# Dividing an attention's rows by their softmax sums behind the value products

## The chip, the core and the metric

The kernel runs on one core of a Trainium2 chip. The core has a matrix engine (TensorE, PE in the profile, with PEld for its weight loads), a vector engine (DVE), an activation engine (ACT), GpSimd (POOL) and a queue that issues most of the DMAs (SP); ACT and POOL issue some too. Sixteen DMA engines move the data. The metric is the device time of one execution in microseconds (us); the kernel before takes 2106.4 us, the median of 3 runs (2104.5 to 2107.51).

## The reference

One encoder layer in float32 is applied to two sequences, a prompt of 1024 tokens and a sample of 512 tokens, with a model width of 1024:

```python
z  = rmsnorm(x) @ w_in          # q_A k_A v_A | q_B k_B v_B | gate_A gate_B
mix = (sigmoid(gate_A) * (o_A @ w_proj_a) + sigmoid(gate_B) * (o_B @ w_proj_b)) @ w_out
h  = x + mix
h  = h + relu(rmsnorm(h) @ w_up)**2 @ w_down
y  = rmsnorm(h)
```

Branch A, which is what changes, is grouped-query attention over all tokens: 8 query heads of 64 columns share 2 key/value heads.

```python
s = einsum('bqkgd,bskd->bkgqs', q, k) * 64**-0.5
p = softmax(s, axis=-1)
o_A = einsum('bkgqs,bskd->bqkgd', p, v)
```

Branch B is attention in a 2-D neighbourhood with a learned bias, and is not touched.

## The kernel before

The two sequences are run one after the other by `run`, first the sample (`NB` = 1 block of 512 queries, tiles named with s0 in the program), then the prompt (`NB` = 2). The multilayer perceptron follows for both together. Matrix products are made in a three-pass form: each operand is split into a high part, rounded to the fast float32 format of TensorE, and a low rest.

For each of the two key/value heads `g`, a stage `phR` makes queries, keys and values, and a stage `phA` makes the attention of the four query heads of that group. Its unit of work is `u = (h, qb)`, a head and a block of 512 queries; there are 8 units in the sample and 16 in the prompt, 24 in all. A unit goes through these steps:

- `s_tile(u, j)`, four times for 128 queries each: two (sample) or four (prompt) matmuls into a score tile in PSUM (lines 801 and 802; there are two such tiles, pool `pbig`), the negated row maximum on DVE (L804), the exponential on ACT with the row sum as a second result (L811), the reciprocal of the sum on DVE (L813), and the division of the whole tile by its sum on POOL (L814). The tile `p` is 128 queries by T keys.
- The tiles are turned, so that keys lie on partitions. In the sample and in the prompt's first query block `t_chunk` does it with four TensorE transposes per 128 keys into a PSUM tile (L838), from which ACT copies the high part (L841) and DVE subtracts it to get the low part (L842). In the prompt's second query block `turn_a` transposes 32 x 32 blocks on DVE (L856) and writes the tile to DRAM (L857, SP), `fetch_a` fetches it turned (L882, SP), and `cut_a` splits it on ACT (L887) and POOL (L889, two halves).
- `pv(u, kc, hi, lo)` multiplies the values with a chunk of 128 keys (lines 825 and 826). The value operand `vhl` holds high and low parts side by side, so its result `o` has 128 rows: 64 of the high part and 64 of the low part, by 512 queries.
- `finish_o`, after the last chunk: ACT copies the lower 64 rows (L484), DVE adds the upper 64 (L494), and `put` stores the sum to the DRAM tensor `oad` by a DMA issued from ACT's queue (L439).

The output of `finish_o` has queries along its 512 columns, while the sums have queries on partitions. `oad` is read again much later, in the projection of branch A (`load_o`, L969).

Work of other kinds is drawn in between by a generator `fill`: `fill.pull(1)` takes one step of the gate products (L214, `gpss`), whose weights are loaded on SP (L247) into three buffers of `rawp` and split on ACT and DVE (L201, L208). The loops of the stage write the order of these calls out by hand; the planner of the tile framework then fixes the order of instructions on each engine from that order, from the dependences, and from costs that it assumes. Once built, every engine's queue is in order: an instruction, or the issue of a DMA, that waits holds all that stands behind it on the same engine.

Of the kernel before, what the change touches and what calls it, by code (L numbers as in the profile page):

```python
# [11 lines left out]
F32 = mybir.dt.float32  # L12
# [3 lines left out]
ALU = mybir.AluOpType  # L16
AX = mybir.AxisListType

P = 128
D = 1024  # L20
NC8 = D // P
HD = 64
# [39 lines left out]
def encoder(ctx: ExitStack, tc: tile.TileContext, xs, outs, w):  # L62
    nc = tc.nc
    dram = ctx.enter_context(tc.tile_pool(name="dram", bufs=1, space=bass.MemoryType.DRAM))
    cst = ctx.enter_context(tc.tile_pool(name="cst", bufs=1))
    sml = ctx.enter_context(tc.tile_pool(name="sml", bufs=8))
# [26 lines left out]
    def mm(name):  # L93
        return pmm.tile([P, 512], F32, tag="mm", name=name)

    def big(name):
        return pbig.tile([P, 1024], F32, tag="big", name=name)
# [325 lines left out]
    def run(tr, nxt, first):  # L423
        N, x, T, NT, NB = tr.N, tr.x, tr.T, tr.NT, tr.NB
        xh, xl = tr.xh, tr.xl
        rows = T // GRID_W
# [4 lines left out]
        oad = dram.tile([4 * P, T], F32, name=f"oad{N}")  # L431
# [5 lines left out]
        def put(dst, src):  # L437
            if slot_no[0] is None:
                nc.scalar.dma_start(dst, src)  # L439
            else:  # L440
                later_put.append((slot_no[0], dst, src))
# [27 lines left out]
                    put(dst[c * P : (c + 1) * P, tb * 512 : tb * 512 + 512], sg)  # L469
                    yield  # L470

        def finish_o(o, n, dst, pool, nm, parts=None):

            both = len(o.shape) == 3
            cols = 2 * n if both else n
            t = pool.tile([P, cols], F32, tag="ot", name=f"ot_{nm}", bufs=2 if cols == 512 and both else 3)
            c, b = t[0:HD, 0:n], t[0:HD, cols - n : cols]
            if both:
                tv = t[0:HD].rearrange("p (i q) -> p i q", i=2)
                nc.scalar.activation(tv, o[HD:P], AF.Copy)  # L480
                nc.vector.tensor_tensor(tv, o[0:HD], tv, op=ALU.add)
                o = b
            else:
                nc.scalar.activation(c, o[HD:P, :n], AF.Copy)  # L484
                o = o[0:HD, :n]
            if parts is not None:
                hi, lo, ps = parts
                b = t[ps, cols - n : cols]
                nc.vector.tensor_tensor(b, o, c, op=ALU.add)
                nc.scalar.activation(hi, b, AF.Copy)  # L490
                op = nc.vector.tensor_tensor(lo, b, hi.bitcast(F32), op=ALU.subtract)
                last_sum[:] = [op.ins]
                return
            nc.vector.tensor_tensor(b, o, c, op=ALU.add)  # L494
            put(dst, b)


# [41 lines left out]
        for g in range(2):  # L539
            with phase(f"phR{N}_{g}") as ph:  # L540
# [175 lines left out]
                for tt in range(NT):  # L716
                    tb, j = divmod(tt, 4)
                    nm = f"{N}_{g}_{tt}"
# [17 lines left out]
                    op = nc.sync.dma_start(rt, w["rope"][tt * P : (tt + 1) * P])  # L736
# [51 lines left out]
                setup_bias()  # L788
            with phase(f"phA{N}_{g}") as ph:
                units = [(h, qb) for h in range(4) for qb in range(NB)]  # L790
                PP = {}

                def s_tile(u, j):
                    h, qb = u
                    nm = f"{N}_{g}_{h}_{qb}_{j}"
                    q0 = (qb * 4 + j) * P
                    lhs = qT[h % 2][:, h // 2, q0 : q0 + P]
                    s = big(f"s{nm}")[:, :T]
                    for kb in range(NB):
                        ks = slice(kb * 512, kb * 512 + 512)  # L800
                        nc.tensor.matmul(s[:, ks], lhs, kT[:, 0, ks], start=True, stop=False)
                        nc.tensor.matmul(s[:, ks], lhs, kT[:, 1, ks], start=False, stop=True)  # L802
                    nm_ = sml.tile([P, 1], F32, tag="nm", name=f"nm{nm}")
                    nc.vector.tensor_reduce(nm_, s, axis=AX.X, op=ALU.max, negate=True)  # L804
                    p = ph.tile([P, T], F32, tag="P", name=f"p{nm}", bufs=8)
                    l = sml.tile([P, 1], F32, tag="l", name=f"l{nm}")
                    to, of = p, s
                    if NB == 2 and qb == 1:
                        to = p.rearrange("p (b k i) -> p k b i", b=4, i=32)
                        of = s.rearrange("p (k i b) -> p k b i", b=4, i=32)  # L810
                    op = nc.scalar.activation(to, of, AF.Exp, bias=nm_, accum_out=l)  # L811
                    rl = sml.tile([P, 1], F32, tag="rl", name=f"rl{nm}")
                    nc.vector.reciprocal(rl, l)  # L813
                    nc.gpsimd.tensor_scalar(p, p, rl, 1.0, op0=ALU.mult, op1=ALU.mult)  # L814
                    PP[u, j] = p
                    return op.ins

                o_of = {}

                def pv(u, kc, hi, lo):  # L820
                    h, qb = u
                    if kc == 0:
                        o_of[u] = mm(f"o{N}_{g}_{h}_{qb}")
                    o = o_of[u]
                    nc.tensor.matmul(o, vhl[:, kc, :], hi, start=(kc == 0), stop=False)
                    nc.tensor.matmul(o, vhl[:, kc, :], lo, start=False, stop=(kc == NT - 1))
                    if kc == NT - 1:
                        r0 = (g * 4 + h) * HD
                        finish_o(o, 512, oad[r0 : r0 + HD, qb * 512 : qb * 512 + 512], ph, f"A{N}_{g}_{h}_{qb}")

                queue = []
                LAG = 2
# [1 line left out]
                def t_chunk(u, kc):  # L834
                    h, qb = u
                    pt = mm(f"pT{N}_{g}_{h}_{qb}_{kc}")
                    for j in range(4):
                        nc.tensor.transpose(pt[:, j * P : (j + 1) * P], PP[u, j][:, kc * P : (kc + 1) * P], ident)  # L838
                    hi = ph.tile([P, 512], F32R, tag="pth", name=f"pth{N}_{g}_{h}_{qb}_{kc}", bufs=3)
# [5 lines left out]
                def next_pv():  # L845
                    if len(queue) > LAG:
                        pv(*queue.pop(0))
# [3 lines left out]
                def turn_a(u, j):  # L851
                    h, qb = u
                    if u not in PD:
                        PD[u] = dram.tile([4, P, T], F32, name=f"ta{N}_{g}_{h}")
                    p = PP.pop((u, j))
                    nc.vector.transpose(p, p)  # L856
                    nc.sync.dma_start(PD[u][j], p)  # L857

                def step_s(u, j):
                    end = s_tile(u, j)  # L860
                    while due:
                        turn_a(*due.pop(0))
                    if u[1]:
                        due.append((u, j))
                    return end
# [25 lines left out]
                if NB == 2:  # L891
# [6 lines left out]
                    for h in range(4):  # L898
                        u, nn, nd = (h, 1), (h + 1, 0), (h + 1, 1)
# [27 lines left out]
                else:  # L927
                    for j in range(4):
                        ends = s_tile(units[0], j)
                        last_exp[:] = [ends]  # L930
                        fill.pull(2)
                    for ui, u in enumerate(units):
                        h, qb = u
# [18 lines left out]
                for item in queue:  # L952
                    pv(*item)
# [85 lines left out]
        with phase(f"phB{N}") as ph:  # L1039
# [4 lines left out]
            n = len(units)  # L1044
# [211 lines left out]
            def v_unit(u):  # L1256
# [27 lines left out]
                if h < 6:  # L1284
                    finish_o(o, nq, obd[h * HD : h * HD + HD, j * nq : (j + 1) * nq], ph, f"B{nm}")
                else:
                    if not oX3:
                        oX3.append(slot([P, 2, T], F32R, f"oX{N}_1_3"))
                    ps = slice(64 * (h % 2), 64 * (h % 2) + 64)
                    hi, lo = (oX3[0][ps, i, j * nq : (j + 1) * nq] for i in range(2))  # L1290
                    finish_o(o, nq, None, ph, f"B{nm}", (hi, lo, ps))
# [18 lines left out]
            for i in range(n + 4 - NB):  # L1310
                if moved:
                    slot_no[0] = i
                if i < n - 8:
                    f = (5 if i < 2 else 2 + i % 2) if NB == 1 else 5 - (i % 6 == 5)
                else:
                    f = 3 if NB == 1 else 8
# [4 lines left out]
                if i < n:  # L1321
# [4 lines left out]
                    h, j = units[i]  # L1326
# [57 lines left out]
        with phase(f"phG{N}") as ph:  # L1384
            oX = load_o(1) + oX3
            wos = [None, None]
            parts = []
# [22 lines left out]
            for c in range(NC8):  # L1410
# [3 lines left out]
                for tb in range(NB):  # L1414
# [4 lines left out]
                    nm = f"{N}_{c}_{tb}"  # L1419
# [30 lines left out]
            for half in range(2):  # L1450
                wo = wos[half]
                hc = slice(half * 512, half * 512 + 512)
                for tt in range(NT):
                    tb, j = divmod(tt, 4)
                    nm = f"{N}_{half}_{tt}"
                    r0 = tr.t0 + tt * P
# [16 lines left out]
                    if half == 0 and NB == 1:  # L1473
# [4 lines left out]
                        o = o4[tt]  # L1478
                    else:
                        o = mm(f"op{nm}")  # L1480
# [27 lines left out]
                    if half == 1:  # L1508
# [12 lines left out]
                        else:  # L1521
# [10 lines left out]
                            if 3 <= tt <= 5:  # L1532
                                j = tt - 3
# [495 lines left out]
    for i, tr in enumerate(trunks):  # L2029
        run(tr, trunks[i + 1] if i + 1 < len(trunks) else None, i == 0)  # L2030
# [66 lines left out]
```

## Time and profile before

| | |
|---|---|
| median of 3 runs | 2106.4 us (2104.5 to 2107.51) |
| profiled execution | 2105.4 us |
| its span in the profile | 2103.6 us |
| POOL busy over the span | 445.6 us (21%) |
| attention of branch A, sample | within 50 to 155 us of the span |
| attention of branch A, prompt | within 440 to 600 and 640 to 765 us |

A row of the profile's groups names the line of the kernel, the engine, the operation, what it writes and reads (`out<-in`), the shapes, the count, the busy time in us and the mean of one in ns; behind that stands how long the engine was idle just before it and what ended that time. In a list of waits each row names who waited for whom, with the total in us, how often, and the longest. In a timeline each row begins with the start and the length in us. Trailing letters of a name stand for numbers left out: `ps` is any probability tile, `pTs` its transpose in PSUM, `os` the product with the values, `hqs` a quarter of a fetched tile, `ptls` and `pths` the low and high parts.

### The profile page before, as it was taken

What the parts mean: (1) busy time and instruction counts of PE and PEld (TensorE: products, weight loads), DVE (VectorE), ACT (ScalarE), POOL (GpSimd) and SP (SyncE); (2) the same over time, 40 slices, a digit from 0 to 9 for tenths busy, and PEclk for the clock granted to TensorE, in tenths of its full rate; (3) what the DMA queues carried; (4) which work ended last, traced back from release to release, by engine and by line L of the source; (5) the groups of instructions that cost most, each with busy time, mean ns of one, the idle gap of its engine ahead of it and who ended that gap; (6) DMA issues with size and microseconds to landing.
All of it is one profiled execution on the core that took longest, in us unless ns stands there. A gap on an engine that the chain in (4) does not pass through costs nothing. (4 is left out here: it accounts for less than half of the span.)

```text
span 2103.6 us, 31314 instructions
## 1 busy us (share of the span) xinstructions
PE 2072.8 (99%) x10615; PEld 1809.0 (86%) x10615; DVE 1477.5 (70%) x2761; ACT 1142.2 (54%) x2455; POOL 445.6 (21%) x510
## 2 busy tenths in 40 slices
PE   9999999999999999999999999999999999999998
PEld 8887878987797778888888999999999988888886
DVE  6665786778648747778854877787777777669563
ACT  6664753667566745566423556565556634334442
POOL 2232310338435823543102100011000000000000
PEclk9999999999999999999999999999999999999999
DMA  6437557557626866877553666478445899788561
GB/s 193 136 101 209 158 165 253 182 135 191 171 65 182 208 170 198 235 225 219 181 182 131 196 195 206 153 240 223 145 155 161 283 342 348 214 273 277 159 209 61
DMA packets 406758, 406.45 MB, mean 193 GB/s; under 512 B 97599, under 2 KB 333767, under 8 KB 406599
## 3 DMA queue, kind: packets, MB, share of 16 engines
q1 hardware_dynamic: 368119, 339.16, 52.8%
q10 hardware_dynamic: 31328, 45.11, 6.4%
q0 software_dynamic: 7152, 20.19, 3.5%
q8 instruction: 84, 1.38, 0.3%
q14 instruction: 75, 0.61, 0.1%
HBM read 291.06 MB, written 114.10 MB: 193 GB/s over the span
## 5 line engine op out<-in xcount | busy, mean ns | idle before, releaser
L214 PE MATMUL dn<-wd,ah 128*128 128x512 f32 x1248 | 384.4, 389 | 0.0
L214 PEld LDWEIGHTS dn<-wd,ah 128*128 128x128 f32 x1248 | 234.2, 188 | 48.7
L214 PE MATMUL dn<-wd,al 128*128 128x512 f32 x624 | 242.8, 389 | 0.0
L1571 ACT ACTIVATE ah<-ar 128x512 fp32r<-128x512 f32 x168 | 104.1, 627 | 203.3 <-PE dn L214 184.3
L214 PE MATMUL gpss<-xs_0h,w_gs 128*128 128x512 f32 x512 | 186.1, 400 | 0.3 <-DVE w_gs L208 0.2
L1572 DVE TENSOR_TENSOR al<-ar,ah 128x512 fp32r<-128x512 f32 x168 | 113.9, 686 | 71.6 <-ACT ah L1571 64.7
L214 PE MATMUL ud<-B,A 128*128 128x384 f32 x768 | 143.6, 334 | 0.7 <-DVE c L1689 0.7
L214 PE MATMUL uc<-B,A 128*128 128x384 f32 x768 | 143.7, 334 | 0.0
L214 PE MATMUL ua<-B,A 128*128 128x384 f32 x768 | 138.8, 334 | 0.0
L214 PEld LDWEIGHTS dn<-wd,al 128*128 128x128 f32 x624 | 117.1, 188 | 24.2
L214 PEld LDWEIGHTS ud<-B,A 128*128 128x128 f32 x768 | 134.0, 188 | 1.1 <-DVE c L1689 1.1
L214 PEld LDWEIGHTS uc<-B,A 128*128 128x128 f32 x768 | 134.1, 188 | 0.2 <-ACT A L1571 0.2
L214 PEld LDWEIGHTS ua<-B,A 128*128 128x128 f32 x768 | 133.7, 188 | 0.2
L180 POOL TENSOR_TENSOR rs_f<-ms_f,mhalf 128x1 f32<-128x1 f32 x6 | 4.0, 667 | 590.7 <-DVE ms_f L176 590.7
L811 ACT ACTIVATE ps<-ss,nms 128x1024 f32<-128x1024 f32 (+1 forms) x96 | 93.4, 973 | 56.4 <-DVE nms L804 46.1
L814 POOL TENSOR_SCALAR ps<-ps,rls 128x1024 f32<-128x1024 f32 (+1 forms) x96 | 97.8, 1019 | 123.6 <-DVE rls L813 105.8
L214 PE MATMUL ops<-wh_os,mgs 128*128 128x512 f32 x384 | 119.5, 391 | 0.0
L804 DVE TENSOR_REDUCE nms<-ss 128x1 f32<-128x1024 f32 (+1 forms) x96 | 99.4, 1038 | 21.7 <-PE ss L802 20.6
L214 PEld LDWEIGHTS gpss<-xs_0h,w_gs 128*128 128x128 f32 x512 | 96.2, 189 | 18.7 <-DVE w_gs L208 0.7
L214 PE MATMUL gpss<-xs_0l,w_gs 128*128 128x512 f32 x256 | 101.2, 395 | 0.0
L1571 ACT ACTIVATE A<-S 128x512 fp32r<-128x512 f32 x128 | 75.9, 624 | 31.7 <-DVE S L1634 22.9
L214 PE MATMUL gpss<-xs_1h,w_gs 128*128 128x512 f32 x256 | 90.8, 393 | 0.0
(299 smaller groups left out, 5160.9 us busy)
## 6 DMA issues: line engine op xcount, KB each, us to landing
ar<-ud SPq DMA_DIRECT2D x120, 512.0 KB, 5.3
br<-in_w_mlp_down_dram SPq DMA_DIRECT2D x72, 512.0 KB, 5.3
rawu<-in_w_mlp_up_dram SPq DMA_DIRECT2D x64, 512.0 KB, 4.1
ud<-c ACTq DMA_DIRECT2D x128, 192.0 KB, 2.6
raw_gs<-in_w_in_dram SPq DMA_DIRECT2D x32, 512.0 KB, 3.9
tas<-ps SPq DMA_DIRECT2D x32, 512.0 KB, 3.1
hqs<-tas SPq DMA_DIRECT2D x32, 512.0 KB, 6.1
ud<-cs SPq DMA_DIRECT2D x64, 192.0 KB
```

The costliest lines, as they stand in the source:

```text
L180: op = nc.gpsimd.tensor_tensor(r[:, :n], m[:, :n], mhalf[:, :n], op=ALU.pow)
L214: op = nc.tensor.matmul(out, a, b, **kw)
L804: nc.vector.tensor_reduce(nm_, s, axis=AX.X, op=ALU.max, negate=True)
L811: op = nc.scalar.activation(to, of, AF.Exp, bias=nm_, accum_out=l)
L814: nc.gpsimd.tensor_scalar(p, p, rl, 1.0, op0=ALU.mult, op1=ALU.mult)
L1571: nc.scalar.activation(hi, src, AF.Copy)
L1572: nc.vector.tensor_tensor(lo, src, hi.bitcast(F32), op=ALU.subtract)
```

## The change

The tiles are no longer divided. The four row sums of a unit go into one tile of four columns, one reciprocal is made of it, and it is written to a DRAM tensor of 4 x 128 values on SP. When the unit's value products begin, the 512 reciprocals are fetched to each of 64 partitions, also on SP, into a tile with two buffers in the sample and one in the prompt. `finish_o` multiplies the sum by that tile on POOL before the store. Branch B calls `finish_o` without it.

```diff
-        def finish_o(o, n, dst, pool, nm, parts=None):
+        def finish_o(o, n, dst, pool, nm, parts=None, scale=None):
...
             nc.vector.tensor_tensor(b, o, c, op=ALU.add)
+            if scale is not None:
+                nc.gpsimd.tensor_tensor(b, b, scale, op=ALU.mult)
             put(dst, b)
...
-                PP = {}
+                PP, L4, rd = {}, {}, {}
...
                     p = ph.tile([P, T], F32, tag="P", name=f"p{nm}", bufs=8)
-                    l = sml.tile([P, 1], F32, tag="l", name=f"l{nm}")
+                    if j == 0:
+                        L4[u] = ph.tile([P, 4], F32, tag="l4", name=f"l{nm}", bufs=4)
+                    l = L4[u][:, j : j + 1]
...
                     op = nc.scalar.activation(to, of, AF.Exp, bias=nm_, accum_out=l)
-                    rl = sml.tile([P, 1], F32, tag="rl", name=f"rl{nm}")
-                    nc.vector.reciprocal(rl, l)
-                    nc.gpsimd.tensor_scalar(p, p, rl, 1.0, op0=ALU.mult, op1=ALU.mult)
                     PP[u, j] = p
+                    if j == 3:
+                        rl = ph.tile([P, 4], F32, tag="r4", name=f"rl{nm}", bufs=3)
+                        nc.vector.reciprocal(rl, L4.pop(u))
+                        rd[u] = dram.tile([4, P], F32, name=f"rd{nm}")
+                        nc.sync.dma_start(rd[u].rearrange("j p -> p j"), rl)
                     return op.ins
...
-                o_of = {}
+                o_of, rb_of = {}, {}
...
                     if kc == 0:
                         o_of[u] = mm(f"o{N}_{g}_{h}_{qb}")
+                        rows = ph.tile([P, 512], F32, tag="rb", name=f"rb{N}_{g}_{h}_{qb}", bufs=3 - NB)
+                        nc.sync.dma_start(rows[0:HD], rd.pop(u).rearrange("j p -> (j p)").partition_broadcast(HD))
+                        rb_of[u] = rows[0:HD]
...
                     if kc == NT - 1:
                         r0 = (g * 4 + h) * HD
-                        finish_o(o, 512, oad[r0 : r0 + HD, qb * 512 : qb * 512 + 512], ph, f"A{N}_{g}_{h}_{qb}")
+                        finish_o(o, 512, oad[r0 : r0 + HD, qb * 512 : qb * 512 + 512], ph, f"A{N}_{g}_{h}_{qb}", None, rb_of.pop(u))
```

## The prediction

> **What bounds the kernel now.** I read the page's head first, then busy time by stage, then the waits of the weight loads, then single stretches of the timeline.
>
> ```profile
> span 2103.6 us, 31314 instructions
> PE 2072.8 (99%) x10615; PEld 1809.0 (86%) x10615; DVE 1477.5 (70%) x2761; ACT 1142.2 (54%) x2455; POOL 445.6 (21%) x510
> ...
> 50.00:155.00 105.00, 103.45 (x572) 87.82 (x571) 70.92 (x155) 68.78 (x194) 30.93 (x42) 1.00 0.39 120
> 440.00:600.00 160.00, 154.07 (x789) 126.14 (x789) 112.40 (x178) 104.48 (x233) 88.59 (x79) 1.00 0.63 162
> 640.00:765.00 125.00, 120.62 (x571) 93.19 (x570) 88.24 (x132) 81.17 (x128) 76.75 (x64) 1.00 0.76 199
> ```
>
> TensorE (PE) is busy nearly everywhere, at full granted clock (1.00, the column ahead of the DMA share). So nothing that another engine saves is worth anything unless it ends a wait of PE. The change lies in branch A's attention, which falls in the three stretches shown (columns: length, then PE, PEld, DVE, ACT, POOL): 50 to 155 us is the sample, the other two are the prompt's two key groups. The rest is not touched. What matters is what PE waits for there:
>
> ```profile
> PE pTs L838 <- POOL ps L814: 2.3, 7, 0.4
> ...
> PEld pTs L838 <- DVE ptls L842: 8.5, 10, 1.8
> PEld ss L801 <- ACT ps L811: 8.1, 20, 1.3
> PEld pTs L838 <- POOL ps L814: 7.8, 16, 0.8
> ...
> PEld os L826 <- DVE ptls L842: 3.8, 7, 0.8
> PEld pTs L838 <- DVE ot_As L494: 2.6, 8, 0.8
> ```
>
> The columns are total us, times, longest. The change takes away what stands in the third PEld row: transposes of the probabilities wait for POOL's division (L814). The matmul row above it gives the same wait 2.3 us, the weight loads give it 7.8. Two stretches show how much time is lost:
>
> ```profile
> 505.70 0.48 PE L825 MATMUL os<-pths,vhls 128*128 128x512 f32 x1
> 506.34 0.19 PEld L826 LDWEIGHTS os<-ptls,vhls 128*128 128x128 f32 x1 [0.48 <-DVE ptls L842]
> 506.34 0.50 PE L826 MATMUL os<-ptls,vhls 128*128 128x512 f32 x1 [0.16 <-DVE ptls L842]
> 506.68 0.40 PE L214 MATMUL gpss<-xs_0h,w_gs 128*128 128x512 f32 x1
> 506.91 0.40 PE L214 MATMUL gpss<-xs_0l,w_gs 128*128 128x512 f32 x1
> ...
> 59.18 0.40 PE L214 MATMUL gpss<-xs_0h,w_gs 128*128 128x512 f32 x1
> 59.70 0.14 PEld L838 LDWEIGHTS pTs<-ident,ps 128*128 128x128 f32 x1 [0.57 <-POOL ps L814]
> 59.71 0.33 PE L838 MATMUL pTs<-ident,ps 128*128 128x128 f32 x1
> ```
>
> Undisturbed, the next matmul starts 0.23 us later (506.68 to 506.91). In the first stall 0.64 passed (505.70 to 506.34): 0.41 lost, where the weight load shows a wait of 0.48 and the matmul 0.16. In the second 0.53 passed: 0.30 lost, of 0.57 shown by the load and nothing by the matmul. Together 0.71 of 1.05, so I count a weight-load wait at 0.68 of its length. The Trainium skill (Perfetto Trace Analysis, Identifying the Most-Contended Engine) says that matmul busy time misleads, because matmuls are pipelined, and that the busy share of the weight loads is to be used; these two stalls agree that the matmul row shows too little, but the load row shows too much. By the matmul row the first term below would be 2.3 us, by the load row 7.8.
>
> **The change, part by part.** Times are set against the profiled execution: 2105.4 us with a span of 2103.6. The median of the runs is 2106.4, so 1.0 is added at the end.
>
> *POOL's division goes out.* These are the steps behind it:
>
> ```profile
> L814 POOL TENSOR_SCALAR ps<-ps,rls 128x1024 f32<-128x1024 f32 (+1 forms) x96 | 97.8, 1019 | 123.6 <-DVE rls L813 105.8
> ...
> L814 POOL TENSOR_SCALAR ps<-ps,rls x96: 691/1119/2002, 53.1 to 731.8; 128x1024 f32<-128x1024 f32 x64, 128x512 f32<-128x512 f32 x32
> ...
> L813 DVE RECIPROCAL rls<-ls x96: 120/152/166, 52.8 to 730.9; 128x1 f32<-128x1 f32 x96
> ...
> DVE rls L813 <- ACT ps L811: 14.7, 16, 1.4
> DVE ps L856 <- POOL ps L814: 10.5, 14, 1.4
> ```
>
> POOL loses 97.8 us, which is worth nothing by itself. Each tile becomes ready for its transposes one reciprocal (0.152) and one pass (1.019 on average, 0.69 in the sample) earlier. The longest stall on it is 0.8, so with the order of PE as it is, every one of these 16 stalls ends: 7.8 x 0.68 = 5.3 us. What is late next is the exponential itself (L811), which comes no earlier. Bounds: 0, if PE's order is planned anew and the transposes are put forward by as much as the chain is shorter, and 5.3. I take 5.3.
>
> *96 reciprocals become 24* of four columns. DVE loses 72 x 0.152 = 10.9 us of work, three quarters of the 14.7 us in which it stood before a reciprocal until the exponential's sum was there (11.0), and most of the 10.5 us in which its block transposes (L856, the prompt's second query block) waited for POOL. That is up to 32.4 us for the engine on which PE waits most in these stages: 8.5 + 3.8 + 2.6 = 14.9 us of load waits, 10.1 after the factor. Per unit (a head and 512 queries, 24 in all) DVE gains 1.35 and PE loses 0.42 to it. Bounds: 0 (the freed time lies behind the stalls) to 10.1. I take half, 5.1, as only relief in front of a stall helps. The 8.1 us for score tiles held by an exponential (5.5 after the factor) I leave at 0, since ACT's own work stays; 5.5 is the bound.
>
> *A product on POOL behind the sum* (24 times, 64 x 512, two inputs). The nearest row is POOL's other two-input pass, the hi/lo cut of the prompt:
>
> ```profile
> L889 POOL TENSOR_TENSOR hqs<-hqs x48: 1271/1292/1737, 470.8 to 739.6; 128x512 fp32r<-128x512 f32 x48
> ...
> L439 ACTq DMA_DIRECT2D oads<-ot_As x24: 452/453/503, 75.1 to 756.8; - x24
> ...
> L484 ACT ACTIVATE ot_As<-os x8: 593/594/596, 670.0 to 755.5; 64x512 f32<-64x512 f32 x8
> ```
>
> It is as long in the free dimension, so 1.29 us each, 31 us in all on an engine that has just lost 98. No matmul reads the product: it goes to DRAM and is read again by the projection much later. But the store sits in ACT's queue (L439), and now waits for POOL instead of DVE; behind it on ACT are exponentials and the hi copies, for which PE waits. The 1.29 itself is a known step that the plan can put other ACT work in front of. What it may miss is that POOL is in a pair of cuts. In the last stretch the cuts are 32 x 1.292 = 41 of 125 us, a third of the time; a third of 16 prompt units with half of a pair (1.3) left is 6.9 us of ACT held. ACT is busy 81.17 of 125 (0.65), so that share is pushed on, and 0.68 of it counts: 3.0 us. In the sample POOL has nothing else and I take 0. Bounds: 0, and a whole pair each time (below, second rival).
>
> *Two DMAs per unit on SP*: 512 single values of 4 bytes out to DRAM, then 2 KB to each of 64 partitions.
>
> ```profile
> vss<-vds SPq DMA_DIRECT2D x128, 32.0 KB, 2.0
> ...
> hqs<-tas SPq DMA_DIRECT2D x32, 512.0 KB, 6.1
> ...
> oads<-ot_As ACTq DMA_DIRECT2D x24, 128.0 KB, 4.2
> ...
> 57.48 0.69 ACT L811 ACTIVATE ps<-ss,nms 128x512 f32<-128x512 f32 x1
> ...
> 72.95 0.59 ACT L484 ACTIVATE ot_As<-os 64x512 f32<-64x512 f32 x1
> ...
> SPq L1073 <- DMA zgs<-sgs: 20.3, 8, 8.6
> ...
> PEld gpss L214 <- DVE w_gs L208: 0.7, 1, 0.7
> ```
>
> The smallest transfers land in 2.0 us. The fetch of 512 KB in runs of 256 bytes is 2048 packets, 128 for each of 16 engines, in 6.1, so a small packet is about (6.1 - 2.0) / 128 = 0.032 us, an estimate. 512 values are 32 per engine, 1.0 us: the row lands after 3.0, the 128 KB to 64 partitions after 4.2 more, 7.2 in all. The first unit's last exponential ends at 58.2 and its sum begins at 73.0, so 14.8 us stand ready. In the prompt, where there is one buffer for the row, the next fetch waits for the product of the unit before; sums come (755.5 - 670.0) / 7 = 12.2 us apart, and product, store slot and fetch are about 6. On the 16 DMA engines 8 units in the last stretch add 8 us to 95 of 125, and the rows a little more: 0.76 becomes about 0.85. The SP queue is in order: a write waits for the reciprocal, a fetch for the write's landing, and behind them stand gate weights, the prompt's block transfers and fetches. Waits of SP for a landing were 2.5 us on average (20.3 / 8). PE waited for gate weights 0.7 us in all, and the three raw buffers ahead of them are the cover; without it 24 holds of 2.5 would be 60 us on SP. I take 0 and let the range carry the rest. The tiles at a stage's end come free some 2 us later, before work that PE does not wait for now: 0.
>
> *Sum*: 2105.4 - 5.3 - 5.1 + 3.0 = 2098.0, and with 1.0 for the median **2099.0 us**.
>
> **The rivals.**
>
> *No change.* The order of PE is planned anew; transposes move forward until they wait for the exponential as they waited for POOL, and DVE's freed time lies behind its stalls. For it: PE already stops 20 times for the exponential in the rows above. Against it: the stalls on POOL are short (0.49 on average) beside what is saved (0.8 to 1.2). The terms vanish and the hold stays: 2106.4 + 3.0 = 2109.4, at best 2102.
>
> *Slower: ACT held at the store.* In each of the 16 prompt units the product comes behind a full pair of cuts, 2 x 1.29 = 2.58 us: 41.3 us of ACT held, x 0.65 x 0.68 = 18.3 instead of 3.0, so 2099.0 + 15.3 = 2114.3. It cancels the gain of 10.4 from 1.5 us of mean hold per prompt unit (10.4 / (16 x 0.65 x 0.68)), and makes the kernel measurably slower from 2.1. For it: POOL is in order and the cuts come in pairs. Against it: POOL loses nearly half of its work in this stage (32 passes of 1.12 out of 76.75), and the store at present is issued with no wait of its own.
>
> *Larger gain.* DVE's relief ends all its stalls: 2106.4 - 5.3 - 10.1 + 3.0 = 2094.0, and if scores stop waiting too and nothing is held, 2106.4 - 20.9 = 2085.5.
>
> *The row comes late.* This needs a packet of 4 bytes to take (14.8 - 2.0 - 4.2) / 32 = 0.27 us, eight times the estimate. At 0.4 it is late by 4.2 us; in the eight sample units alone, x 0.66 x 0.68, that is 15 us, so about 2114. The Trainium skill (DMA: Bandwidth & Descriptors, Rules for kernel authors) speaks against this write: a strided last dimension becomes one descriptor per element, and its Specifications add that transfers under 512 bytes are done by read-modify-write. No run here shows such a write yet.
>
> That the change doesn't do what it says can be excluded: the 96 passes leave the program.
>
> **How the numbers follow.** About 0.2% (4.2 us) is what a measurement of this kernel can tell from no change. Forecast (2094 to 2102) 0.42; larger gain 0.16; no change (2102 to 2110.6) 0.23; held store 0.16; late row 0.03. So faster 0.58, same 0.23, slower 0.19. The range 2086 to 2112 leaves out the last of the larger gain (0.04) and most of the two slower cases (0.14). The forecast's own range is 2094 to 2102.
>
> **What would show it.** Right: no wait of the transposes on POOL, weight-load waits on DVE in the three stretches down by about half, POOL's time down by some 65 us, PE's order in the stretches much the same. Wrong: the wait of transposes on the exponential grown by what the other lost; ACT's next instruction behind an L439 store late with POOL in its cuts; the 64-partition row landing after the sum; gate matmuls waiting for their weights.

## The result, and the profile after

The changed kernel takes 2237.65 us (median of 6 runs, 2224.43 to 2249.34), the kernel before beside it 2106.3 (6 runs, 2104.5 to 2107.51). The ratio is 1.0617, with a 95% interval of 1.0578 to 1.0656: slower by 131 us, where 7 us less was forecast and 2112 was the end of the range. The profiled execution took 2237.52 us.

First the head of the page after, then the three windows that were shown before (columns: length, PE, PEld, DVE, ACT, POOL, granted clock, DMA share, GB/s). The attention now runs later, its last product starts at 886.3 us, so these windows don't hold the same work as before:

```profile
span 2235.7 us, 31184 instructions
...
PE 2112.1 (94%) x10615; PEld 1841.8 (82%) x10615; DVE 1471.3 (66%) x2689; ACT 1143.3 (51%) x2455; POOL 380.8 (17%) x438
```

```profile
50.00:155.00 105.00, 91.74 (x479) 78.15 (x478) 51.49 (x103) 53.01 (x158) 14.20 (x16) 0.93 0.44 106
440.00:600.00 160.00, 133.46 (x705) 112.61 (x704) 99.98 (x154) 91.42 (x234) 45.18 (x44) 0.93 0.72 117
640.00:765.00 125.00, 112.29 (x631) 101.37 (x632) 64.08 (x120) 64.61 (x218) 31.46 (x36) 0.94 0.53 105
```

The span grew by 132.1 us, in two parts. TensorE was idle for 123.6 us (2235.7 - 2112.1) instead of 30.8 (2103.6 - 2072.8), 92.8 more. And the same 10615 matmuls were busy 39.3 us longer: the granted clock is 0.93 to 0.94 in these windows, where it was 1.00. The DMA moved less in them (106, 117 and 105 GB/s instead of 120, 162 and 199) although in the first two its engines were marked busy for a larger share. The idle time of PE has other names than before. These are the waits of the weight loads:

```profile
PEld pTs L847 <- DVE ptls L851: 32.0, 11, 7.5
PEld ss L803 <- ACT ps L815: 26.6, 18, 6.3
PEld os L834 <- ACT pths L850: 24.3, 9, 3.6
PEld pTs L847 <- ACT sgs L468: 12.5, 2, 6.4
PEld os L834 <- DVE ptls L851: 8.9, 2, 5.5
```

The transposes (`pTs`) no longer wait for POOL, as forecast. But single waits are now up to 7.5 us long where none of the rows before was above 1.8, and they end on ACT and DVE. What ACT in turn waited for most is a transfer. The longest waits of ACT and of SP for transfers, in the stretch from 50 to 900 us:

```profile
ACT hqs L896 <- DMA hqs<-tas: 81.0, 19, 8.1
```

```profile
SPq L891 <- DMA tas<-ps: 73.5, 9, 12.5
SPq L831 <- DMA rds<-rls: 66.2, 11, 9.4
```

In the kernel before, ACT waited 0.9 us in all for the fetch of a turned tile (`hqs`), and this was SP's wait for the write ahead of it (`tas`):

```profile
SPq L882 <- DMA tas<-ps: 20.0, 9, 2.9
```

Both come late now, and neither is touched by the change. The fetch of the row (L831) waits up to 9.4 us for the row's write. The first unit shows how it goes. These are rows of the timeline after:

```profile
59.17 0.38 SPq L821 DMA_DIRECT2D rds<-rls  x1
59.65 1.52 SPq L507 DMA_DIRECT2D rawqs<-in_w_in_dram  x1
...
70.93 0.48 SPq L831 DMA_DIRECT2D rbs<-rds  x1
...
73.16 1.06 ACT L201 ACTIVATE wghs<-rawqs 128x1024 fp32r<-128x1024 f32 x1 [4.88 <-DMA rawqs<-in_w_in_dram]
```

and the windows of the same time (columns as above):

```profile
60.00:62.00 2.00, 2.00 (x12) 1.59 (x11) 1.66 (x4) 1.76 (x4) 0.00 (x0) 1.00 0.13 3
62.00:64.00 2.00, 2.00 (x12) 1.70 (x11) 1.82 (x4) 2.00 (x7) 0.00 (x0) 1.00 0.14 16
64.00:66.00 2.00, 2.00 (x14) 1.65 (x12) 1.23 (x3) 1.24 (x3) 0.00 (x0) 1.00 0.37 45
66.00:68.00 2.00, 2.00 (x12) 1.65 (x11) 1.26 (x4) 1.09 (x2) 0.00 (x0) 1.00 0.46 29
68.00:70.00 2.00, 2.00 (x12) 1.68 (x11) 1.36 (x3) 0.29 (x2) 0.00 (x0) 1.00 0.46 20
...
72.00:74.00 2.00, 0.00 (x0) 0.00 (x0) 0.00 (x0) 0.84 (x1) 0.00 (x0) 0.90 0.91 247
...
76.00:78.00 2.00, 2.00 (x6) 1.61 (x5) 1.43 (x3) 0.64 (x2) 0.00 (x0) 0.50 0.80 53
```

The write of 512 single values is issued at 59.17, and behind it a fetch of 512 KB of weights, `rawqs`. The write's own packets are no burden:

```profile
DMA packets 773, 0.27 MB, mean 22 GB/s; under 512 B 528, under 2 KB 772, under 8 KB 772
```

These are the DMA packets from 59 to 71 us. The 528 small ones, 512 values and 16 more, all run between 60.0 and 61.1, about the 1.0 us that was forecast for them. But then the DMA moves 3 to 45 GB/s until 70, although the fetch is waiting; in the kernel before it moved 257 and 252 GB/s from 60 to 64. A store of 256 KB that ACT issued at 62.98 on its own queue moved no packet before 71 either. The row is fetched at 70.93, 11.8 us after its write was issued (forecast: 3.0). ACT starts on the weights at 73.16, after a wait of 4.88 for that transfer. PE has nothing to do from 72 to 74. Then the clock is granted at 0.50, and 2 us hold 6 matmuls instead of 12. So the loss is made of two things: a transfer that stands still, and the clock that falls after the idle time.

### The profile page after: what moved, and what is told of

Its sections match the earlier page's. It is cut to its first block, busy times and chain, and to the rows that moved or that the text cites. A ratio compares the mean times of both kernels' runs of the same rounds, so it can differ in the third digit from the quotient of the medians.

```text
span 2235.7 us, 31184 instructions
## 1 busy us (share of the span) xinstructions
PE 2112.1 (94%) x10615; PEld 1841.8 (82%) x10615; DVE 1471.3 (66%) x2689; ACT 1143.3 (51%) x2455; POOL 380.8 (17%) x438
## 5 line engine op out<-in xcount | busy, mean ns | idle before, releaser
L214 PE MATMUL gpss<-xs_0h,w_gs 128*128 128x512 f32 x512 | 191.8, 413 | 1.1 <-ACT sgs L468 0.6
L847 PE MATMUL pTs<-ident,ps 128*128 128x128 f32 x384 | 70.2, 307 | 49.6 <-DVE ptls L851 31.9
L847 PEld LDWEIGHTS pTs<-ident,ps 128*128 128x128 f32 x384 | 54.2, 159 | 68.8 <-DVE ptls L851 32.0
L851 DVE TENSOR_TENSOR ptls<-pTs,pths 128x512 fp32r<-128x512 f32 x96 | 63.2, 679 | 68.7 <-ACT pths L850 68.3
```

The costliest lines, as they stand in the source:

```text
L214: op = nc.tensor.matmul(out, a, b, **kw)
L851: nc.vector.tensor_tensor(lo, pt, hi.bitcast(F32), op=ALU.subtract)
```

## The experiments

Three theories were set against each other. A: the writes of 4 bytes hold up everything on the 16 DMA engines. B: it is the queues, SP waiting for the row's landing and ACT at the store behind POOL's product. C: the planner's new order of the work is worse. A difference in us below is between a kernel and the kernel before, measured beside it on the same chip, unless another is named. The cuts of code show the lines that matter; `...` stands for what is left out.

**The row in runs of 16 bytes.** The change with one thing altered: the DRAM row is laid out query by query, so that the four values of a partition are one run. The product reads the fetched row in that order.

```diff
...
-rd[u] = dram.tile([4, P], F32, name=f"rd{nm}")
-nc.sync.dma_start(rd[u].rearrange("j p -> p j"), rl)
+rd[u] = dram.tile([P, 4], F32, name=f"rd{nm}")
+nc.sync.dma_start(rd[u], rl)
...
```

> The row of reciprocals is written as 128 runs of 16 bytes (one per partition) instead of 512 values of 4 bytes; POOL's product reads it in the permuted order. Everything else is the changed kernel (2237.65 us, 131 over the kernel before). Theory A (the small writes themselves hold up the 16 DMA engines for some 10 us each time, in proportion to their number): the loss falls to about a quarter, 2125 to 2150. Theory B (the waits in the queues: SP until the row has landed, ACT at the store until POOL's product is done, whatever the write looks like): over 2200. Theory C (the planner's new order without POOL's division): 2238.

Measured: 2109.15 us (2107.44 to 2110.91, 10 runs), ratio 1.0015 (1.0005 to 1.0024). All but 3.2 us of the loss is gone, more than A had expected, with every queue, fetch and product of the change in place. By the two traces PE, DVE, POOL and SP run the same instructions in the same order in this kernel and in the changed one, so the new order isn't the cause: C falls.

**The write alone.** The kernel before with the 24 writes added, which nobody reads; for this the four reciprocals of a unit stand in one tile, `R4`.

```diff
...
+rd = dram.tile([4, P], F32, name=f"rd{nm}")
+nc.sync.dma_start(rd.rearrange("j p -> p j"), R4.pop(u))
```

> The kernel before, with its division on POOL, and in addition the 24 writes of 512 values of 4 bytes, which nobody reads. Theory A: most of the loss is there, 2180 to 2240. Theory B: only SP's wait for the reciprocals is added, 2106 to 2115. Theory C: 2106.

Measured: 2206.36 us (2202.83 to 2211.18), ratio 1.048 (1.0461 to 1.0499). Writes on which nothing waits cost 100.4 us, 4.2 for each. A stands and B falls as the main cause.

**The change without the write.** The fetch reads 512 constants in its place.

```diff
-rd[u] = dram.tile([4, P], F32, name=f"rd{nm}")
-nc.sync.dma_start(rd[u].rearrange("j p -> p j"), rl)
...
-nc.sync.dma_start(rows[0:HD], rd.pop(u).rearrange("j p -> (j p)").partition_broadcast(HD))
+src = w["norm_final_g"]
+nc.sync.dma_start(rows[0:HD], bass.AP(tensor=src.tensor, offset=src.offset, ap=[[0, HD], [1, 512]]))
```

> The changed kernel without the write: the row fetched to 64 partitions is 512 values of an input, so the output is multiplied by those and not divided by the sums. The product on POOL, the wait of the store for it and the single row buffer are all there. Theory A: the loss is gone, 2095 to 2110. Theory B: SP's wait for the landing is gone, ACT's hold at the store stays, 2130 to 2200. Theory C: 2238.

Measured: 2108.71 us (2106.47 to 2112.34), ratio 1.0016 (1.0007 to 1.0026). It is within half a microsecond of the row in runs of 16 bytes. So a row written in such runs, and the wait for its landing, cost next to nothing. The planner gave this kernel an order of its own (514 of PE's 10615 matmuls stand elsewhere than in the changed kernel), so it says little about C.

**No division at all.** No reciprocals, no row, no product: the sums are left out.

```diff
-nc.vector.reciprocal(rl, L4.pop(u))
...
-nc.sync.dma_start(rd[u].rearrange("j p -> p j"), rl)
...
-nc.sync.dma_start(rows[0:HD], rd.pop(u).rearrange("j p -> (j p)").partition_broadcast(HD))
...
-finish_o(o, 512, ..., None, rb_of.pop(u))
+finish_o(o, 512, ...)
```

> The changed kernel without any division: no reciprocals, no row, no product, so the sums are left out of the result. It is the most that the change could win. By the prediction's terms 2086 to 2096 (5.3 to 20.9 us below the kernel before). Theories A and B: the same. Theory C: over 2200.

Measured: 2090.42 us (2090.14 to 2091.07), ratio 0.9927 (0.9911 to 0.9944). The most that the change could gain is 15.6 us. Its weight loads wait less, for the exponential and for the low parts, than they did before (8.1 and 8.5):

```profile
PEld ss L803 <- ACT ps L815: 4.3, 17, 0.4
...
PEld pTs L841 <- DVE ptls L845: 3.2, 5, 1.6
```

**What about the 4 bytes?** The next kernels have the unread writes again, in other forms, to tell the number of writes from their place in DRAM. In four of them, all but the one with 128 values, PE, DVE, POOL and SP run in the same order as with the write alone, so that only the form of the write differs. First, each value at the start of its own 64 bytes:

```diff
...
+rd = dram.tile([4, P, 16], F32, name=f"rd{nm}")
+nc.sync.dma_start(rd[:, :, 0].rearrange("j p -> p j"), R4.pop(u))
```

> As the run with the write alone (the kernel before and 24 unread writes of 512 values of 4 bytes, 2206.36 us against 2105.98), but each value goes to the start of its own 64 bytes in DRAM, so that no two share such a stretch. Theory A1 (what is slow is neighbours written in pieces into one short stretch of DRAM, by one engine after another): the loss goes, 2106 to 2120. Theory A2 (the number of small writes alone): 2190 to 2220 as before.

Measured: 2103.07 us (2101.28 to 2103.8), ratio 0.9986 (0.9977 to 0.9995). 512 writes of 4 bytes don't lengthen the kernel if they lie this far apart, and neither does the order of work that the added writes bring. Second, 256 runs of 8 bytes:

```diff
...
+rd = dram.tile([2, P, 2], F32, name=f"rd{nm}")
+nc.sync.dma_start(rd.rearrange("a p b -> p a b"), R4.pop(u).rearrange("p (a b) -> p a b", a=2))
```

> As the run with the write alone, but 256 runs of 8 bytes in place of 512 of 4. 512 runs cost 100 us; 128 runs of 16 bytes cost about nothing (2109.15 with the row against 2108.71 without the write). If the cost is in proportion to the number of runs: about 2156. If there is a threshold between: near 2106 or near 2206.

Measured: 2109.95 us (2106.89 to 2111.87), ratio 1.0019 (1.001 to 1.0028), 4.3 us more. Third, each value at the start of its own 8 bytes:

```diff
...
+rd = dram.tile([4, P, 2], F32, name=f"rd{nm}")
+nc.sync.dma_start(rd[:, :, 0].rearrange("j p -> p j"), R4.pop(u))
```

> The kernel before with the same 24 unread writes of 512 values of 4 B, each value now at the start of its own 8 bytes (4 KB of DRAM per write in place of 2 KB). At a distance of 4 bytes the writes cost 100 us (2206.4), at 64 bytes nothing (2103.1). Theory S (it costs when many values share one short stretch of DRAM): eight values share 64 bytes here, in place of sixteen, so it still costs, by about half: some 2150, and 2130 to 2206. Theory C (it costs when two 4-byte values lie right against each other, in one 8-byte word): nothing, 2100 to 2112.

Measured: 2109.1 us (2106.36 to 2114.07, 10 runs), ratio 1.0017 (1.0008 to 1.0026). Eight values share 64 bytes here, and it costs 3.2 us, not 50: theory S fails by its figure, and C (two values in one word of 8 bytes) keeps its own. The same moment as above, in this kernel, first its timeline and then its windows:

```profile
59.06 0.38 SPq L820 DMA_DIRECT2D rds<-r4s  x1
59.53 1.36 SPq L505 DMA_DIRECT2D rawqs<-in_w_in_dram  x1
...
68.39 1.05 ACT L201 ACTIVATE wghs<-rawqs 128x1024 fp32r<-128x1024 f32 x1
```

```profile
60.00:62.00 2.00, 2.00 (x12) 1.69 (x13) 1.43 (x4) 2.00 (x6) 0.69 (x1) 1.00 0.14 5
62.00:64.00 2.00, 2.00 (x13) 1.66 (x12) 1.86 (x5) 1.93 (x5) 0.69 (x1) 1.00 0.38 59
64.00:66.00 2.00, 2.00 (x13) 1.64 (x12) 1.37 (x4) 1.40 (x4) 1.39 (x2) 1.00 0.90 316
```

From 60 to 64 the DMA is nearly still here too (5 and 59 GB/s, against 257 and 252 in the kernel before). But then the weights come at 316 GB/s, and ACT takes them up at 68.39 without waiting for them. So this write also holds up the fetch, for some 4 us in place of some 10, and that much was covered. The median time from the write's issue to its landing, read from the traces, goes up in steps as well: 1.7 us in runs of 16 bytes, 2.0 at a distance of 64, 4.1 in runs of 8 bytes, 4.4 at a distance of 8, and 8.0 for the fifth form below. So a small loss in the kernel's time says that little had to wait, not that nothing was held up.

Fourth, only 128 of the 512 values, one against the other:

```diff
...
+rd = dram.tile([1, P], F32, name=f"rd{nm}")
+nc.sync.dma_start(rd.rearrange("j p -> p j"), R4.pop(u)[:, 0:1])
```

> The kernel before with 24 unread writes of only the first 128 values of a unit, 4 B each, one against the other (512 B of DRAM per write). If each small write has a price of its own, a quarter of 100 us: 2125 to 2137. If the price is of a backlog that only builds up with 512 of them at once: 2103 to 2112.

Measured: 2162.98 us (2161.7 to 2167.91), ratio 1.0275 (1.026 to 1.0291). A quarter of the writes costs 57.1 us, over half of the whole: both expectations missed. The price is neither in proportion to the number nor a backlog that needs 512 of them. The order of PE differs here from that with 512 values at 336 places, so a part of the 57.1 may belong to that.

Fifth, 512 values one against the other, but neighbours in DRAM now come from the same partition (against the write alone):

```diff
-R4[u] = ph.tile([P, 4], F32, tag="r4", name=f"r4{nm}", bufs=4)
-rl = R4[u][:, j : j + 1]
+R4[u] = ph.tile([P, 8], F32, tag="r4", name=f"r4{nm}", bufs=4)
+rl = R4[u][:, 2 * j : 2 * j + 1]
...
-rd = dram.tile([4, P], F32, name=f"rd{nm}")
-nc.sync.dma_start(rd.rearrange("j p -> p j"), R4.pop(u))
+rd = dram.tile([P, 4], F32, name=f"rd{nm}")
+nc.sync.dma_start(rd, R4.pop(u).rearrange("p (j two) -> p j two", two=2)[:, :, 0])
```

> The kernel before with 24 unread writes of 512 values that lie one against the other in DRAM, 2 KB per write, as in the costly ones (2206.4), but in the other order: the four values of one partition are neighbours, taken from every second column of a tile of eight, so that they cannot be joined to a run of 16 B. If the price comes with 4-byte pieces that lie one against the other, whoever writes them: 2190 to 2210. If it comes only where the neighbours are written from different partitions, and so at different moments: 2100 to 2112.

Measured: 2179.16 us (2177.11 to 2187.23), ratio 1.0358 (1.0333 to 1.0383). 73.7 us: less than the 100.4 of the other order, but far above the free forms. It lies between the two expectations, much nearer to the first. So the price doesn't need neighbours from different partitions, although that order is 26.7 us dearer. What the dear forms share, and none of the cheap ones has, is two 4-byte pieces in one word of 8 bytes. But in the same forms every second piece also starts in the middle of such a word, if the tensor begins at the start of one, and in the cheap forms none does. No run tells these two apart: single values in second halves alone were not tried.

**The last 18 us.** With the row in runs of 16 bytes the kernel is 18.7 us above the one without division. The held store of the second rival would explain it: ACT does wait for POOL's product there.

```profile
ACT ps L820 <- POOL ot_As L496: 12.7, 8, 2.0
...
ACT pths L855 <- POOL ot_As L496: 9.9, 5, 2.6
```

So the store was taken from ACT's queue and issued by POOL itself:

```diff
...
+nc.gpsimd.dma_start(dst, b)
+return
```

> The changed kernel with runs of 16 bytes (2109.15 us), with the stores of branch A's output issued from POOL's queue, behind the product, and not from ACT's. 18.7 us lie between that kernel and the one without any division (2090.42). Theory B1 (ACT held at the store until POOL's product is done): most of it comes back, 2091 to 2098. Theory B2 (SP held at the fetch until the single row buffer is free again): 2105 to 2110, no change. Theory B3 (what is left is the planner's order): 2105 to 2112.

Measured: 2110.55 us (2108.94 to 2112.68), ratio 1.0023 (1.0014 to 1.0032). Nothing is gained, although ACT waits for no product any more. This doesn't quite free the held store of its charge: the 24 issues now stand in POOL's queue, 14.0 us in all, ahead of its other work. Beside it, with the store back in its place, the product was moved to DVE:

```diff
-nc.gpsimd.tensor_tensor(
+nc.vector.tensor_tensor(
...
```

> The changed kernel with runs of 16 bytes (2109.15 us), with the product on DVE behind its own sum and not on POOL; the store stays on ACT's queue. Theory B1: the hop to POOL and its queue are gone from in front of the store, and 24 x 0.68 = 16 us come on DVE; 2095 to 2103. Theory B2: the row buffer comes free earlier too, 2095 to 2105, so that this run tells B1 and B2 apart only together with the store on POOL. Theory B3: 2105 to 2115.

Measured: 2098.32 us (2097.16 to 2099.13), ratio 0.9964 (0.9951 to 0.9978). That is 10.8 us better than the row in runs of 16 bytes, and better than the kernel before. The timeline of the kernel with POOL's store shows what the product on POOL does:

```profile
552.12 1.95 POOL L496 TENSOR_TENSOR ot_As<-ot_As,rbs 64x512 f32<-64x512 f32 x1 [1.23 <-DVE ot_As L494]
552.57 7.87 DVE L208 TENSOR_TENSOR wgls<-rawqs,wghs 128x512 fp32r<-128x512 f32 x2
...
554.95 4.93 POOL L905 TENSOR_TENSOR hqs<-hqs 128x512 fp32r<-128x512 f32 x4
560.36 1.27 DVE L858 TENSOR_TENSOR ptls<-pTs,pths 128x512 fp32r<-128x512 f32 x2
...
561.09 1.11 PE L854 MATMUL pTs<-ident,ps 128*128 128x128 f32 x4 [5.81 <-DVE ptls L858]
```

The product holds back POOL's cuts, which then run as four in a row. DVE's subtract of two SBUF tiles beside them (L208) takes 7.87 us for two, where one takes 0.67 to 0.68. The low part (`ptls`) comes behind it, and PE stands for 5.81 us. The groups of that line in this kernel and in the one with the product on DVE (min/median/max in ns):

```profile
L208 DVE TENSOR_TENSOR wgls<-rawqs,wghs x12: 670/682/5883, 70.0 to 561.6; 128x512 fp32r<-128x512 f32 x12
```

```profile
L208 DVE TENSOR_TENSOR wgls<-rawqs,wghs x12: 671/683/1757, 70.3 to 550.1; 128x512 fp32r<-128x512 f32 x12
```

The Trainium skill (GPSIMD Engine Reference, 1. Specifications) says that GpSimd shares its SBUF interfaces with VectorE and collides with instructions of two SBUF inputs; these rows agree. What the runs show is that 10.8 us go with the engine of the product, together with the hold at the store and with the order that the planner makes of it (PE's order differs at 428 places between the two kernels of the comparison). How they divide was not tried. Theory B2, SP held at the fetch until the row buffer is free, fits both times too. By the traces that wait goes down only from 39.3 to 31.1 us in all with the product on DVE, and ACT waits no less for the turned tiles that stand behind it in SP's queue (2.2 and 2.4 us), so it is an unlikely cause. In the trace of the kernel with runs of 16 bytes the stall at L208 is there too: PE stands for 4.33 us. And there is a second one: PE stands for 2.61 us up to 125.05, with the granted clock at 0.50 from 126 to 130, where the kernel with the product on DVE stands for 1.53 us and keeps its full clock.

**The change in the prompt alone.** The best kernel so far, with the sample's 8 units divided on POOL as before.

```diff
...
+if NB == 1:
+    rl = sml.tile([P, 1], F32, tag="rl", name=f"rl{nm}")
+    nc.vector.reciprocal(rl, l)
+    nc.gpsimd.tensor_scalar(p, p, rl, 1.0, op0=ALU.mult, op1=ALU.mult)
...
```

> The kernel with the row in runs of 16 B and the product on VectorE (2098.3), with the change only for the prompt's 16 units; the sample's 8 units divide their tiles on GpSimd as before. If the change gains in the prompt alone, because there the matmuls wait for GpSimd's divisions, and the sample's part is a loss by its row and product: 2093 to 2097. If it gains in both: 2099 to 2103.

Measured: 2094.49 us (2093.81 to 2096.06, 5 runs), ratio 0.9947 (0.9935 to 0.996). The sample's part was a loss of 3.8 us. This is the fastest version with the division in it, 11.4 us below the kernel before.

## Why the prediction was wrong

**The step that failed** is "Two DMAs per unit on SP", with its "I take 0". The price of a 4-byte write was worked out from a fetch of 256-byte runs, at 0.032 us a packet, and the harms weighed were a row late for its own reader and an SP queue held until the landing. The packets were priced well: 33 for each of 16 engines ran in about 1 us, 0.03 us each. What the sum left at nothing, and nowhere names, is what the write does to the transfers behind it on the DMA engines. Measured, the write costs 100.4 us in the kernel before, where nobody waits for it, and 128.5 in the changed one (2237.65 - 2109.15): 4.2 and 5.4 us for each of 24, seen as other transfers that stand still and as half clock after them. The fetch of the row was not measured by itself; together with the other remains of the change, and without the costly write, the kernel is at 2108.7, 2.7 us above the kernel before.

**The late row** had the right place, a 4-byte packet, and the wrong mechanism: it asked for 0.27 us a packet, let the row be late by itself and came to 2114. The row was late, its fetch is issued 11.8 us after its write, but its packets were not slow, and PE waited for weights, turned tiles and what follows from them. The Trainium skill (DMA: Bandwidth & Descriptors, Specifications) gives 512 bytes as the least size for line rate, with a read-modify-write below it. The runs agree in that small writes can be dear, but size alone doesn't set the price here: 4-byte writes at a distance of 8 or 64 bytes cost 3.2 us and nothing.

**POOL's division out**, 5.3: the wait of the transposes on POOL is gone after. This part held, as far as a wait shows it: without the division the transposes wait 0.6 us in all for the exponential in its place.

**DVE's relief**, 5.1 taken of 10.1, and scores at 0 of 5.5: too small in all. The whole gain without division is 15.6 us, not 10.4, inside the bound of 20.9; the waits shown above fall there from 8.1 to 4.3 and from 8.5 to 3.2. How the 15.6 divide among the three terms no run shows.

**The product on POOL**, 3.0: its length was right, 1.28 us in the median:

```profile
L496 POOL TENSOR_TENSOR ot_As<-ot_As,rbs x24: 1253/1280/2253, 79.8 to 886.3; 64x512 f32<-64x512 f32 x24
```

Its price was not: 10.8 us against the same product on DVE, measured in a form that reads the row with a stride and takes 1.54 us in the median. The held store has 18.3 where 18.7 were left, but that is luck: the hold is real, moving the store away gained nothing, and a part of the price is seen where POOL runs beside DVE, which the prediction did not think of. For the sample 0 was taken for the hold, and the whole change there, with the product on DVE, costs 3.8.

**The sum, with measured terms**: 2106.0 - 15.6 for the division left out, + 4.1 for the row and a product on DVE in the prompt, with the sample's division left as it was (2094.49 - 2090.42), + 3.8 for the sample's part, + 10.8 for the product on POOL, + 128.5 for the write in single values, is 2237.6. Each term is the difference of two neighbouring kernels, so the sum has to come out; it shows where the time goes and is no proof of the causes. The terms come from different sets of runs, in which the kernel before was within 0.6 us.

**PE's order** was said to stay much the same. It did not: the planner put the attention's instructions in another order from the first units on. The kernel with the row in runs of 16 bytes has the same order as the changed one, and so shows that this isn't what cost.

**Open**: why the price is not in proportion (57.1 us for 128 values, 100.4 for 512); whether it comes from two pieces in one word or from a piece that starts in the middle of one; and where in the path to DRAM the transfers are held.

## What to carry to other kernels

A transfer's own packets can be cheap and the transfer dear, by what it does to the others. No row of the trace before shows that when the kind of access is new; measure such a transfer by itself, added unread to the kernel before, and look at what the other transfers do meanwhile. Lay small results out in runs of at least 8 bytes, or leave single values 8 bytes or more apart: 24 such writes cost 4.3 us or less here. A step moved from one engine to another should be asked what runs beside it on the shared paths, not only how long it takes.

## What the runs showed of the hardware

- Writes of 4 bytes that lie one against the other, two to a word of 8 bytes, hold up the other transfers: each write of 512 of them made the kernel 4.2 us longer, of 128 of them 2.4 us. The packets themselves were through in about 1 us. In runs of 8 or 16 bytes, or at a distance of 8 or 64 bytes, the cost is between nothing and 0.2 us a write, although at a distance of 8 the fetch behind is held for some 4 us.
- The clock fell after short idle times. In the kernel with the product on DVE, PE was idle for 2.03 us up to 552.5, and for 0.67 us shortly before, and this is the next window:

```profile
554.00:556.00 2.00, 2.00 (x11) 1.70 (x10) 1.14 (x2) 1.18 (x2) 0.20 (x1) 0.55 0.60 209
```

  In the kernel with the change in the prompt alone, gaps of 0.82 and 2.03 us at the same place were followed by a granted clock of 1.00. The Trainium skill (TensorE: Matmul & The Clock Gate, Part 1: The HAM clock gate) speaks of an idle window of about 3.4 us that runs free. That like gaps end differently agrees with its running free; that the clock fell after 2.03 us, with 0.67 shortly before, doesn't fit 3.4 us as a safe length.
- Where GpSimd's passes of two inputs met a DVE subtract of two SBUF inputs, DVE paid most: one subtract went from 0.68 to 5.88 us. The four cuts beside it took 1.2 us each (4.93 / 4), the product ahead of them 1.95 against a median of 1.55.
